# First modulation blocks split between TensorE and VectorE in a planned decoder block, with other costs in its planner

## The chip, the cores and the metric

The kernel runs on one core of a Trainium2 chip. The core has five instruction queues: TensorE (PE, matrix products; its weight loads are shown as PEld), VectorE (DVE), ScalarE (ACT), GpSimd (POOL) and SyncE (SP, which here only issues DMAs). Each queue works through its instructions in the order in which they were written; queues wait for one another by semaphores. The metric is the device time of one execution in microseconds, lower is better: the median of several runs.

## The reference

One decoder layer on 512 tokens of width 1024, all in float32, with one conditioning vector `c`:

```python
c_act = jax.nn.silu(c)
mod = c_act @ w_ada[l] + b_ada[l]                       # 1024 -> 6 * 1024
shift1, scale1, gate1, shift2, scale2, gate2 = split(mod, 6)
h = rms_norm(x, g_pre_mix[l]) * (1.0 + scale1) + shift1
y = token_mixer(h, ...)                                 # z = h @ w_in; conv branch, attention branch, merge
x = x + gate1 * rms_norm(y, g_post_mix[l])
h = rms_norm(x, g_pre_mlp[l]) * (1.0 + scale2) + shift2
y = square(relu(h @ w_mlp_in[l])) @ w_mlp_out[l]        # 1024 -> 4096 -> 1024
x = x + gate2 * rms_norm(y, g_post_mlp[l])
```

The six parts of `mod` are each a product of one vector of 1024 with a 1024 x 1024 matrix. Parts 0 and 1 (shift1, scale1) are needed before the first projection of the mixer can start, part 5 (gate2) only at the very end.

## The kernel before

All large products run on TensorE as three products of a split: each float32 operand is cut into a high part (rounded to float32r by a copy) and a low part (operand minus high part), and high x high, high x low, low x high are summed in PSUM (`mm3`, and the triple loop in `first_products`). So each weight block costs one copy on ScalarE (CAST in the profile) and one subtraction on VectorE (TENSOR_TENSOR), made by the class `W`, before its last third can run.

**The start of the kernel** is what most of the change touches. `x` comes in four row tiles of 512 KB; each is squared and summed on ScalarE, its reciprocal root is taken on GpSimd (a power of -0.5), and VectorE scales it. TensorE transposes the result in 32 blocks of 128 x 128 (4 per feature block, 8 feature blocks `k`), into one PSUM bank per feature block, and a copy brings each bank to `xnT`: the copies of the feature blocks in `XDVE` (L43; 1, 3, 5, 7) are on VectorE, those of the others on ScalarE (L636). The vector `c` is loaded after x, transposed on TensorE and turned into silu(c), the eight columns `cT`.

Then, for each of the eight feature blocks `k`, the kernel needs 128 columns of shift1 and of scale1. `ada_load` (L544) brings a block of 1024 x 2 x 128 weights (1 MB in 512-byte rows) by four DMAs of 256 KB. For `k` = 0 and 1 the sum over the 1024 inputs is made on TensorE, by eight float32 matmuls each with one column of `cT` as the weights (M = 1, N = 256); the row that comes out is copied by ScalarE and turned into columns by two more small matmuls and a transfer on VectorE (`to_columns`, L657). For `k` = 2 to 7 (the groups of `KGRP`) VectorE makes the sum: one TENSOR_SCALAR and seven SCALAR_TENSOR_TENSOR of 128 x 256, and `to_columns` then also adds over the partitions, with a vector of ones. `first_products` (L669) makes the modulated feature block (high part on ScalarE; a full-precision copy `v` on VectorE for `k` < `VDVE` = 2 and on ScalarE for the rest; low part on VectorE), splits the block of `w_in` that `g1_load` (L558) brought (128 rows x 896 columns, two DMAs), and issues 21 matmuls of 128 x 512 into seven PSUM banks.

**Late modulation.** Parts 2, 3, 4 and 5 are summed on VectorE beside other work, by the generator `ada_units` (L1167). A unit is one DMA of 1 MB and two VectorE instructions of 128 x 1024. `take(late, n)` advances it by n units. Part 5 (four units) is taken in the MLP. The MLP works in four quarters `ch` of 1024 hidden units (L1657); in each, the hidden units come in groups, most of them by a Strassen scheme (`strassen_in`), and their product with `w_mlp_out` by another (`strassen`). Before the change part 5 is taken from quarter 2 on: two units after each of the Strassen groups of that quarter (L1668), so all four units in quarter 2.

**What sets the order.** The program is first recorded as a list of operations (`record`), and then a list scheduler (`Planner.plan`, L325) simulates it with a cost for each operation (`cost`, L234, and a DMA's time in `record`). It decides the order in which each queue gets its instructions; this order is fixed in the program. TensorE takes the ready operation with the lowest rank, which is the place in the recorded list less `plan.boost`. The other queues take the ready operation with the earliest due time less `plan.hurry`. Due times are counted back from TensorE's order. `region` (L199) says which parts of a buffer an operation touches, as a range from the lowest to the highest word. Placement in the two SBUF arenas (`f_arena`, `r_arena`) and in the PSUM banks follows the simulated lifetimes, over up to 14 passes, and the pass with the shortest simulated length is issued. A buffer that is given to a new load must first be free, so placement also makes waits. The simulation holds SP back so that no more than `DEPTH` = 8 DMAs are under way.

All recorded instructions carry the line of one helper, L410, so groups of instructions are told apart by tiles and shapes.

Of the kernel before, what the change touches and what calls it, by code (L numbers as in the profile page):

```python
# [17 lines left out]
P = 128  # L18
# [23 lines left out]
CONV_DVE = ((0, 1), (2, 3), (4, 5), (6, 7))  # L42
XDVE = (1, 3, 5, 7)  # L43
VDVE = 2
TAIL = 2e4
# [6 lines left out]
ADAS = (1, 1, 0, 4)  # L52
KGRP = ((2,), (3,), (4,), (5,), (6,), (7,))
HX, HA, HG, HC = 1.2e5, 1e5, 3e3, 1.1e5
# [115 lines left out]
class Planner:  # L170
# [27 lines left out]
    @staticmethod  # L198
    def region(ap):  # L199

        t = ap.tensor
        dims = [list(d) for d in ap.ap]
        name = t.name.split("_bitcast")[0]
        row = dims[0][0]
        if row == 0 or len(t.shape) < 2 or "dram" in name or "spill" in name:
            return name, range(ap.offset, ap.offset + 1)
        if name.startswith("rows"):
            return name, range(ap.offset // row, ap.offset // row + dims[0][1])
        lo = ap.offset % row
        hi = lo + sum((n - 1) * s for s, n in dims[1:])  # L210
        u = 256 if name.startswith("psum") else 8 if "arena" in name else 1
        return name, range(lo // u, hi // u + 1)

# [20 lines left out]
    def cost(self, eng, fn, outs, ins, k):  # L234
# [17 lines left out]
        if eng == "dve":  # L252
            if fn in ("tensor_copy", "tensor_scalar"):
                return (1.04 if psum else 0.52) * n + 68 + 61 * scalars, 150.0
            if fn == "scalar_tensor_tensor":
                return 1.04 * n + 130, 150.0
            return 1.04 * n + 70, 150.0
        if fn == "memset":
            return 36.0, 100.0
        return (460.0 if ALU.pow in self.args else 160.0) + 1.0 * n, 150.0  # L260

    def record(self, eng, fn, a, k):
# [18 lines left out]
        if fn == "dma_start":  # L281
# [3 lines left out]
            n = min(self.run(outs[0]), self.run(ins[0]), 4096)  # L285
            o.dma = b * (13.0 + 0.0385 * n) / (16 * n) * (2 if eng == "pool" else 1)
        deps = set()
# [37 lines left out]
    def plan(self):  # L325
# [13 lines left out]
        heaps = {e: [] for e in self.NAMES}  # L339
        free = {e: 0.0 for e in self.NAMES}  # L340
        dma_free = 0.0
        landed = [0.0] * DEPTH
# [72 lines left out]
def tile_hybrid_block(  # L415
# [48 lines left out]
    def emit(past, replay):  # L464
# [72 lines left out]

        plan.hurry = HC
        c8 = tile_of([8, P], F32, "c8")
# [3 lines left out]

        def ada_load(ks):  # L544

# [3 lines left out]
            src = w_ada.rearrange("(j p) (s n) -> p s j n", p=P, s=6)  # L549
            step = KD // 2  # L550
            for j in range(0, KD, step):
                for s in range(2):
                    sp.dma_start(out=v[:, s, j:j + step], in_=src[:, s, j:j + step, ks[0] * P:ks[0] * P + n])
# [16 lines left out]
        plan.hurry = HA  # L570
        ada0 = ada_load((0,))
        plan.hurry = 0.0
# [83 lines left out]

        def to_columns(src, lp, ks):  # L657

            for s in range(2):
                for i, k in enumerate(ks):  # L660
                    pe.matmul(pb.v(bg)[:, s * KD + k:s * KD + k + 1], lhsT=src[:, s, i * P:(i + 1) * P], rhs=ones[0:lp, 0:1],
                              start=True, stop=True)
            ksl = slice(ks[0], ks[-1] + 1)
# [24 lines left out]

        plan.boost = 1000
        ad0 = [ada0]  # L690
        plan.hurry = HA - 1e4
        ad0.append(ada_load((1,)))
        wbs = []
        for k in range(2):
            plan.hurry = HA - (5e3 if k == 0 else 1.5e4)
            wbs.append(g1_load(k))
        plan.hurry = HG
        for k in range(2):
            av = ad0[k][1]
            ro = pb.v(bg)[0:1, 256:512].rearrange("p (s n) -> p s n", s=2)  # L700
            for j in range(KD):
                pe.matmul(ro, lhsT=cT[:, j:j + 1], rhs=av[:, :, j], start=j == 0, stop=j == KD - 1)
            fa.free(ad0[k][0])
            acc = fa.alloc(2 * P)
            accv = fa.v(acc, "p (s n) -> p s n", s=2)[0:1]
            act.copy(accv, ro)
            to_columns(accv, 1, (k,))
            fa.free(acc)
        plan.boost = 0
        plan.hurry = 0.0  # L710
        for k in range(2):
            first_products(k, wbs[k])

        for ks in KGRP:
            plan.hurry = HA - 1e4 * ks[0]
            n = len(ks) * P
            ab, av = ada_load(ks)
            ada_end = len(plan.ops) - 1
# [3 lines left out]
            plan.boost = 1000  # L722
            acc = fa.alloc(2 * n)
            accv = fa.v(acc, "p (s n) -> p s n", s=2)
            for j in range(KD):
                if j == 0:
                    dve.tensor_scalar(accv, av[:, :, 0], cT[:, 0:1], None, ALU.mult)
                else:
                    dve.scalar_tensor_tensor(accv, av[:, :, j], cT[:, j:j + 1], accv, op0=ALU.mult, op1=ALU.add)
            fa.free(ab)  # L730
            to_columns(accv, P, ks)
            fa.free(acc)
            plan.boost = 0
            plan.hurry = 0.0
            for k, wb in zip(ks, wbs):
# [921 lines left out]
        for ch in range(NCH):  # L1657
# [3 lines left out]
            for n0 in range(0, HPC, GRP):  # L1661
                if (ch, n0 - n0 % 4) in SIN:
                    if n0 % 4 == 0:
                        if not h2s_:
                            h2_sums()
                        strassen_in(hv, n0, (ch * HPC + n0) * P)
                        if ch >= NCH - 2:
                            take(late, 2 * ADAS[1])  # L1668
# [14 lines left out]
                for i in range(GRP):  # L1683
# [4 lines left out]
                    pb.free(bs[i])  # L1688
                if ch >= NCH - 2:
                    take(late, ADAS[1])  # L1690
# [110 lines left out]
```

## Time and profile before

| quantity | value |
|---|---|
| median of three runs | 815.28 us (814.91 to 816.14) |
| the profiled execution's own time | 812.54 us |
| its span, first to last instruction | 810.4 us |
| mean granted TensorE clock | 0.998 |
| TensorE matmul busy | 790.7 us, 4450 instructions |
| VectorE busy | 738.0 us |
| ScalarE busy | 472.0 us |
| GpSimd busy | 62.8 us |
| bytes moved by DMA | 131.00 MB, mean 162 GB/s |

Times in the views count from the start of the span. `out<-in` names the buffers that an instruction writes and reads; `128*1 128x256` on a matmul is the shape of its weights and of its moving operand. A float32 matmul is recorded as two instructions, a float32r matmul as one. Buffers of an arena all have the arena's name. "Idle before" is the time for which the engine stood still ahead of a group, with what ended it. A busy TensorE is not a TensorE at its peak, since the ends of matmuls are modelled: the number of matmuls in a stretch tells more.

### The profile page before, as it was taken

What the parts mean: (1) busy time and instruction counts of PE and PEld (TensorE: products, weight loads), DVE (VectorE), ACT (ScalarE), POOL (GpSimd) and SP (SyncE); (2) the same over time, 40 slices, a digit from 0 to 9 for tenths busy, and PEclk for the clock granted to TensorE, in tenths of its full rate; (3) what the DMA queues carried; (4) which work ended last, traced back from release to release, by engine and by line L of the source; (5) the groups of instructions that cost most, each with busy time, mean ns of one, the idle gap of its engine ahead of it and who ended that gap; (6) DMA issues with size and microseconds to landing.
All of it is one profiled execution on the core that took longest, in us unless ns stands there. A gap on an engine that the chain in (4) does not pass through costs nothing. (4 is left out here: it accounts for less than half of the span.)

```text
span 810.4 us, 11974 instructions
## 1 busy us (share of the span) xinstructions
PE 790.7 (98%) x4450; PEld 687.7 (85%) x4450; DVE 738.0 (91%) x1045; ACT 472.0 (58%) x784; POOL 62.8 (8%) x121
## 2 busy tenths in 40 slices
PE   6999999999999999999999999999999999999996
PEld 3778988889897888888888879988998899889985
DVE  3898999999999999999997579899689999996997
ACT  5455463365885247229243378677667756777851
POOL 2001010000000000000000021001002200320023
PEclk9999999999999999999999999999999999999999
DMA  9989433112352160064998044159317991895076
GB/s 295 313 247 341 144 116 110 53 53 66 105 170 78 53 202 5 1 222 162 344 391 281 7 159 148 53 149 266 132 53 157 243 343 37 171 288 178 28 164 134
DMA packets 99981, 131.00 MB, mean 162 GB/s; under 512 B 8433, under 2 KB 67154, under 8 KB 99922
## 3 DMA queue, kind: packets, MB, share of 16 engines
q1 hardware_dynamic: 93586, 118.69, 45.1%
q0 software_dynamic: 6336, 11.54, 8.9%
q8 instruction: 35, 0.57, 0.3%
q14 instruction: 24, 0.20, 0.1%
HBM read 109.23 MB, written 20.97 MB: 161 GB/s over the span
## 5 line engine op out<-in xcount | busy, mean ns | idle before, releaser
L410 PE MATMUL psum<-r_arena 128*128 128x512 f32 (+3 forms) x4108 | 751.1, 344 | 4.0 <-DVE f_arena L410 1.6
L410 PEld LDWEIGHTS psum<-r_arena 128*128 128x128 f32 x4108 | 647.6, 189 | 91.7 <-ACT r_arena L410 2.7
L410 ACT CAST r_arena<-f_arena 128x1024 fp32r<-128x1024 f32 (+5 forms) x249 | 235.2, 966 | 137.3 <-PE psum L410 86.4
L410 DVE TENSOR_TENSOR r_arena<-f_arena,r_arena 128x1024 fp32r<-128x1024 f32 (+5 forms) x259 | 276.1, 1093 | 28.0 <-PE psum L410 15.1
L410 DVE SCALAR_TENSOR_TENSOR f_arena<-f_arena,cw 128x512 f32<-128x512 f32 x240 | 164.2, 737 | 0.0
L410 DVE TENSOR_TENSOR f_arena<-f_arena 128x1024 f32<-128x1024 f32 (+3 forms) x108 | 113.6, 1071 | 4.7 <-ACT f_arena L410 2.4
L410 ACT ACTIVATE f_arena<-f_arena 128x512 f32<-128x512 f32 (+4 forms) x121 | 71.3, 607 | 42.9 <-DVE f_arena L410 42.0
L410 ACT COPY f_arena<-psum 128x512 f32<-128x512 f32 (+4 forms) x103 | 55.3, 547 | 41.5 <-PE psum L410 36.9
L410 DVE SCALAR_TENSOR_TENSOR f_arena<-f_arena,cT 128x256 f32<-128x256 f32 (+1 forms) x70 | 55.9, 800 | 1.2
L410 POOL DMA_DIRECT2D y_spill<-f_arena x40 | 34.8, 879 | 263.6 <-ACT f_arena L410 254.8
L410 ACT ACTIVATE f_arena<-psum 128x512 f32<-128x512 f32 x43 | 25.2, 593 | 45.4 <-PE psum L410 44.3
L410 PE MATMUL psum<-ident,f_arena 128*128 128x128 f32 (+1 forms) x234 | 34.8, 288 | 7.9 <-DVE f_arena L410 7.9
L410 PEld LDWEIGHTS psum<-ident,f_arena 128*128 128x128 f32 (+1 forms) x234 | 28.3, 147 | 14.0 <-DVE f_arena L410 9.3
L410 ACT CAST r_arena<-psum 128x512 fp32r<-128x512 f32 (+2 forms) x57 | 30.0, 562 | 12.7 <-PE psum L410 12.4
L410 DVE TENSOR_TENSOR r_arena<-psum,r_arena 128x512 fp32r<-128x512 f32 (+2 forms) x57 | 35.6, 653 | 0.9 <-ACT r_arena L410 0.6
L410 DVE TENSOR_TENSOR f_arena<-psum,f_arena 128x512 f32<-128x512 f32 (+1 forms) x34 | 22.3, 666 | 7.7 <-PE psum L410 7.6
L410 POOL TENSOR_TENSOR stats<-stats,nhalf 128x1 f32<-128x1 f32 (+1 forms) x17 | 15.5, 915 | 172.3 <-ACT stats L410 156.3
L410 POOL TENSOR_TENSOR lns<-lns,nhalf 128x4 f32<-128x4 f32 x1 | 1.4, 1400 | 249.5 <-DVE lns L410 249.5
L410 ACT ACTIVATE r_arena<-f_arena 128x256 fp32r<-128x256 f32 (+3 forms) x17 | 10.9, 642 | 14.4 <-DVE f_arena L410 11.3
L410 ACT ACTIVATE r_arena<-f_arena,mod 128x512 fp32r<-128x512 f32 x8 | 6.5, 816 | 21.6 <-DVE mod L410 21.6
L410 DVE TENSOR_SCALAR f_arena<-f_arena,stats 128x1024 f32<-128x1024 f32 x8 | 6.0, 753 | 13.6 <-POOL stats L410 13.6
L410 DVE CUSTOM_DVE_ANT_0 f_arena<-psum,mask 128x128 f32<-128x128 f32 (+3 forms) x32 | 14.6, 481 | 0.0
(98 smaller groups left out, 211.1 us busy)
## 6 DMA issues: line engine op xcount, KB each, us to landing
f_arena<-in_w_ada_dram SPq DMA_DIRECT2D x16, 1024.0 KB
f_arena<-in_w_mlp_in_dram SPq DMA_DIRECT2D x32, 512.0 KB
f_arena<-in_w_mlp_out_dram SPq DMA_DIRECT2D x32, 512.0 KB
f_arena<-in_w_in_dram SPq DMA_DIRECT2D x24, 512.0 KB
y_spill<-f_arena POOLq DMA_DIRECT2D x40, 256.0 KB, 6.2
f_arena<-in_w_ada_dram SPq DMA_DIRECT2D x32, 256.0 KB
f_arena<-in_x_dram SPq DMA_DIRECT2D x8, 512.0 KB
h_spill<-r_arena SPq DMA_DIRECT2D x16, 256.0 KB
```

The costliest lines, as they stand in the source:

```text
L410: getattr(self.real[o.eng], o.fn)(*o.a, **o.k)
```

## The change

Seven things are changed.

1. The sums of feature blocks 0 and 1 are shared. A new function `ada_sums` gives the weight rows `j` in `PE0` = 0, 2, 4, 6 (block 0) and `PE1` = 0, 1, 2 (block 1) to TensorE and the others (1, 3, 5, 7 and 3 to 7) to VectorE. `to_columns` takes a list of sources and adds them in PSUM, so it has four matmuls in place of two for these blocks. Blocks 2 to 7 keep the sum on VectorE. Block 1 moves into the common loop, so TensorE's part of it stands behind block 0's products in the recorded list, and only its `to_columns` is boosted.
2. `ada_load` for blocks 0 and 1 issues eight DMAs of 128 KB (one for each `j`, both halves) instead of four of 256 KB.
3. `c` is loaded ahead of x.
4. `XDVE` is empty and `VDVE` is 0: all eight copies of transposed x, and the full-precision modulated blocks 0 and 1, are on ScalarE.
5. The planner's costs of a 128 x 256 SCALAR_TENSOR_TENSOR, of the power on GpSimd, and of DMAs (plain and accumulating) are changed, and SP starts at 750 ns in the simulation.
6. `region` splits a strided access into its pieces, so that operations on different pieces are no longer taken to depend on one another.
7. `LATE5` = 1: part 5 is taken from quarter 1 on, so its four units are taken in quarter 1.

```diff
-XDVE = (1, 3, 5, 7)
-VDVE = 2
+XDVE = ()
+VDVE = 0
+PE0, CH0, PE1, CH1 = (0, 2, 4, 6), 1, (0, 1, 2), 1
+H1 = 3e3
+BOOST0 = 1000
+H0 = 2e4
-KGRP = ((2,), (3,), (4,), (5,), (6,), (7,))
+KGRP = ((1,), (2,), (3,), (4,), (5,), (6,), (7,))
+ADD, LATE5 = 2.6, 1
@@ region
-        hi = lo + sum((n - 1) * s for s, n in dims[1:])
         u = 256 if name.startswith("psum") else 8 if "arena" in name else 1
-        return name, range(lo // u, hi // u + 1)
+        at, inner = [lo], dims[1:]
+        while len(inner) > 1 and inner[0][0] >= 128 and inner[0][1] * len(at) <= 64:
+            s, n = inner.pop(0)
+            at = [a + i * s for a in at for i in range(n)]
+        ext = sum((n - 1) * s for s, n in inner)
+        return name, sorted({v for a in at for v in range(a // u, (a + ext) // u + 1)})
@@ cost, record, plan
-                return 1.04 * n + 130, 150.0
+                return 1.04 * n + (200 if n == 256 else 130), 150.0
-        return (460.0 if ALU.pow in self.args else 160.0) + 1.0 * n, 150.0
+        return (820.0 if ALU.pow in self.args else 160.0) + 1.0 * n, 150.0
-            o.dma = b * (13.0 + 0.0385 * n) / (16 * n) * (2 if eng == "pool" else 1)
+            o.dma = b * (6.0 + 0.040 * n) / (16 * n) * (ADD if eng == "pool" else 1)
+        free["sp"] = 750.0
@@ loads
-        plan.hurry = HC
+        plan.hurry = HX + 1e4
         c8 = tile_of([8, P], F32, "c8")
-        def ada_load(ks):
+        def ada_load(ks, step=KD // 2):
...
+                if step == 1:
+                    sp.dma_start(out=v[:, :, j], in_=src[:, 0:2, j, ks[0] * P:ks[0] * P + n])
+                    continue
-        ada0 = ada_load((0,))
+        ada0 = ada_load((0,), 1)
@@ sums
-        def to_columns(src, lp, ks):
+        def to_columns(srcs, ks):
             for s in range(2):
                 for i, k in enumerate(ks):
+                    for src, lp in srcs:
+                        pe.matmul(pb.v(bg)[:, s * KD + k:s * KD + k + 1], lhsT=src[:, s, i * P:(i + 1) * P],
+                                  rhs=ones[0:lp, 0:1], start=src is srcs[0][0], stop=src is srcs[-1][0])
+        plan.hurry = HA - 1e3
+        wbs = [g1_load(0)]
+        ro = pb.v(bg)[0:1, 256:512].rearrange("p (s n) -> p s n", s=2)
+        def ada_sums(ks, ada, on_pe=(), chains=1):
+            n = len(ks) * P
+            ab, av = ada
+            srcs, bufs = [], []
+            if on_pe:
+                bufs.append(fa.alloc(2 * P))
+                srcs.append((fa.v(bufs[0], "p (s n) -> p s n", s=2)[0:1], 1))
+            sums = []
+            at = 0
             for j in range(KD):
+                aj = av[:, :, j]
+                if j in on_pe:
+                    pe.matmul(ro, lhsT=cT[:, j:j + 1], rhs=aj, start=j == on_pe[0], stop=j == on_pe[-1])
+                    continue
+                if len(sums) < chains:
+                    bufs.append(fa.alloc(2 * n))
+                    sums.append(fa.v(bufs[-1], "p (s n) -> p s n", s=2))
+                    dve.tensor_scalar(sums[-1], aj, cT[:, j:j + 1], None, ALU.mult)
+                else:
+                    q = sums[at % chains]
+                    dve.scalar_tensor_tensor(q, aj, cT[:, j:j + 1], q, op0=ALU.mult, op1=ALU.add)
+                at += 1
+            fa.free(ab)
+            if on_pe:
+                act.copy(srcs[0][0], ro)
+            plan.boost = 1000
+            to_columns(srcs + [(q, P) for q in sums], ks)
+            fa.free(*bufs)
+            plan.boost = 0
+            plan.hurry = 0.0
+        plan.boost = BOOST0
+        plan.hurry = H0
+        ada_sums((0,), ada0, PE0, CH0)
+        first_products(0, wbs[0])
         for ks in KGRP:
             plan.hurry = HA - 1e4 * ks[0]
-            ab, av = ada_load(ks)
+            ada = ada_load(ks, 1 if ks[0] == 1 and PE1 else KD // 2)
...
+            if ks[0] == 1:
+                plan.hurry = H1
+                ada_sums(ks, ada, PE1, CH1)
+            else:
+                ada_sums(ks, ada)
@@ MLP, both places
-                        if ch >= NCH - 2:
+                        if ch >= LATE5:
                             take(late, 2 * ADAS[1])
```

More of the change, by code (lines that the diff above doesn't have):

```diff
@@ L549, in ada_load @@
             src = w_ada.rearrange("(j p) (s n) -> p s j n", p=P, s=6)
-            step = KD // 2
             for j in range(0, KD, step):
+                if step == 1:
+                    sp.dma_start(out=v[:, :, j], in_=src[:, 0:2, j, ks[0] * P:ks[0] * P + n])
+                    continue
                 for s in range(2):
@@ L655, in emit @@
         bg = bc
-        def to_columns(src, lp, ks):
+        def to_columns(srcs, ks):
             for s in range(2):
                 for i, k in enumerate(ks):
-                    pe.matmul(pb.v(bg)[:, s * KD + k:s * KD + k + 1], lhsT=src[:, s, i * P:(i + 1) * P], rhs=ones[0:lp, 0:1],
-                              start=True, stop=True)
+                    for src, lp in srcs:
+                        pe.matmul(pb.v(bg)[:, s * KD + k:s * KD + k + 1], lhsT=src[:, s, i * P:(i + 1) * P],
+                                  rhs=ones[0:lp, 0:1], start=src is srcs[0][0], stop=src is srcs[-1][0])
             ksl = slice(ks[0], ks[-1] + 1)
@@ L686, in first_products @@
             w.free()
[L689 to L700, printed above, removed]
-            for j in range(KD):
[L702 to L712, printed above, removed]
+        plan.hurry = HA - 1e3
[10 more added lines that the diff above has]
+            at = 0
+            for j in range(KD):
+                aj = av[:, :, j]
[18 more added lines that the diff above has]
+            plan.hurry = 0.0
@@ L714, in emit @@
+        plan.boost = BOOST0
+        plan.hurry = H0
+        ada_sums((0,), ada0, PE0, CH0)
+        first_products(0, wbs[0])
         for ks in KGRP:
             plan.hurry = HA - 1e4 * ks[0]
-            n = len(ks) * P
-            ab, av = ada_load(ks)
+            ada = ada_load(ks, 1 if ks[0] == 1 and PE1 else KD // 2)
             ada_end = len(plan.ops) - 1
@@ L722, in emit @@
             plan.boost = 1000
[L723 to L734, printed above, removed]
+            if ks[0] == 1:
[3 more added lines that the diff above has]
+                ada_sums(ks, ada)
             for k, wb in zip(ks, wbs):
@@ L1688, in emit @@
                     pb.free(bs[i])
-                if ch >= NCH - 2:
+                if ch >= LATE5:
                     take(late, ADAS[1])
```

## The prediction, made before the changed kernel was run

> **What bounds the kernel now.** I read the page first, then the engines' busy time by stretch, then TensorE's instructions in order of time.
>
> ```profile
> span 810.4 us, 11974 instructions
> PE 790.7 (98%) x4450; PEld 687.7 (85%) x4450; DVE 738.0 (91%) x1045; ACT 472.0 (58%) x784; POOL 62.8 (8%) x121
> ...
> 0.00:12.00 12.00, 4.59 (x20) 3.80 (x21) 2.89 (x8) 7.28 (x15) 5.14 (x49) 1.00 0.89 280
> 12.00:24.00 12.00, 11.62 (x59) 5.55 (x57) 6.85 (x11) 5.25 (x9) 0.75 (x2) 1.00 1.14 318
> 24.00:64.00 40.00, 39.91 (x186) 31.90 (x186) 36.92 (x82) 18.03 (x24) 0.68 (x6) 1.00 0.98 284
> 260.00:280.00 20.00, 20.00 (x90) 16.58 (x89) 20.00 (x28) 5.77 (x7) 0.00 (x0) 1.00 0.26 76
> 540.00:600.00 60.00, 60.00 (x405) 55.75 (x404) 48.81 (x44) 41.34 (x53) 3.50 (x5) 1.00 0.61 181
> 620.00:680.00 60.00, 58.90 (x400) 54.73 (x399) 55.95 (x52) 40.58 (x52) 8.39 (x10) 1.00 0.84 240
> 800.00:812.00 12.00, 2.79 (x22) 2.38 (x20) 6.52 (x14) 0.81 (x3) 1.55 (x2) 0.82 0.65 147
> ```
>
> The columns of the stretches are length, then PE, PEld, DVE, ACT and POOL busy with counts, granted clock, DMA share, GB/s. TensorE is idle for 19.7 us in all (810.4 - 790.7), 7.4 of them before its first instruction, so what shortens the kernel is less work on TensorE or an earlier start of useful work. At its best it runs 90 matmuls in 20 us (260 to 280), 222 ns each. Here is its beginning:
>
> ```profile
> 7.41 1.76 PE L410 MATMUL psum<-ident,f_arena 128*128 128x128 f32 x7 [7.41 <-DVE f_arena L410]
> 13.30 3.61 PE L410 MATMUL psum<-f_arena,cT 128*1 128x256 f32 x16
> 17.65 0.60 PE L410 MATMUL psum<-ones,f_arena 1*128 1x1 f32 x4
> 18.18 0.59 PE L410 MATMUL psum<-f_arena,cT 128*1 128x256 f32 x2
> 20.80 1.89 PE L410 MATMUL psum<-f_arena,cT 128*1 128x256 f32 x8
> 22.62 1.20 PE L410 MATMUL psum<-r_arena 128*128 128x512 f32 x4
> 24.27 7.10 PE L410 MATMUL psum<-r_arena 128*128 128x512 f32 x30
> 31.58 5.52 PE L410 MATMUL psum<-r_arena 128*128 128x512 f32 x23
> 53.06 0.50 PE L410 MATMUL psum<-ones,f_arena 128*128 128x1 f32 x4
> 53.42 5.19 PE L410 MATMUL psum<-r_arena 128*128 128x512 f32 x21
> 58.45 0.50 PE L410 MATMUL psum<-ones,f_arena 128*128 128x1 f32 x4
> 58.81 6.79 PE L410 MATMUL psum<-r_arena 128*128 128x512 f32 x27
> ```
>
> The first product runs at 22.62; until then TensorE does transposes and 16 modulation matmuls (32 records). 34 of the 168 first products are done at 31.4, so block 1's last (the 42nd) is done near 33.4 (8 more at 0.25 us). From there each feature block takes 5.39 us (53.06 to 58.45), where 21 matmuls at 222 ns and the 0.36 us of the transfer (53.06 to 53.42) would be 5.02: these matmuls take 247 ns, with VectorE busy 36.92 of 40 us. The eighth block ends near 64.1 (21 of the last 27). Behind it TensorE has hardly a gap, and one that bears on the change, at 661.64, is below.
>
> **1. The shared sums, on TensorE.** Nine of sixteen modulation matmuls leave TensorE. Eight took 3.61 us, so that is -4.06 us. Each of blocks 0 and 1 gets two more small matmuls in the transfer; two take 0.53 us (17.65 to 18.18), so +1.06. Net -3.0 us of TensorE work: with TensorE full from 12 us on, the lower bound of the gain, if nothing else moves.
>
> **2. The same, as a chain.** The start is earlier by more than that, because block 1's matmuls now stand behind block 0's products and no longer ahead of them (20.80 to 22.62). I build block 0's new chain from these rows:
>
> ```profile
> 0.74 1.81 SPq L410 DMA_DIRECT2D f_arena<-in_x_dram  x4
> 2.60 0.39 SPq L410 DMA_DIRECT2D c<-in_c_dram  x1
> 8.15 0.37 SPq L410 DMA_DIRECT2D f_arena<-in_w_ada_dram  x1
> 9.77 0.92 SPq L410 DMA_DIRECT2D f_arena<-in_w_ada_dram  x2
> SPq L410 <- DMA f_arena<-in_x_dram: 4.0, 4, 2.1
> 4.39 1.06 ACT L410 ACTIVATE r_arena<-f_arena 128x1024 fp32r<-128x1024 f32 x1 [2.06 <-DMA f_arena<-in_x_dram]
> 29.71 1.00 DVE L410 SCALAR_TENSOR_TENSOR f_arena<-f_arena,cT 128x256 f32<-128x256 f32 x2
> 32.07 0.82 ACT L410 ACTIVATE r_arena<-f_arena,mod 128x512 fp32r<-128x512 f32 x1 [5.65 <-DVE mod L410]
> 32.79 0.80 ACT L410 ACTIVATE f_arena<-f_arena,mod 128x512 f32<-128x512 f32 x1
> ```
>
> SP waits four times for tiles of x: its ninth DMA is issued only when an earlier one lands, so eight are in flight. Its issues at 8.15 and 9.77 follow the third and fourth tile of x. With c ahead, x lands about 0.4 later (0.39 for c's issue): the last tile at 10.2. Block 0's 1.05 MB at 318 GB/s take 3.3 us more, 13.5. Its pieces are half as large, so eight in flight hold less; after the last tile of x lands three pieces have still to be issued, for which I add 0.5: 14.0. VectorE's last sum takes 0.5, and from the end of a sum to the modulated block on ScalarE it is 1.36 us (30.71 to 32.07), then 0.82: first product near 16.9, against 22.62.
>
> **3. ScalarE's load** goes against this. Empty `XDVE` and `VDVE` = 0 give it work that VectorE did:
>
> ```profile
> 13.08 1.07 ACT L410 COPY f_arena<-psum 128x512 f32<-128x512 f32 x2 [1.83 <-PE psum L410]
> 19.91 1.76 ACT L410 CAST r_arena<-f_arena 128x896 fp32r<-128x896 f32 x2
> 22.78 0.36 ACT L410 COPY f_arena<-psum 1x256 f32<-1x256 f32 x1 [1.10 <-PE psum L410]
> 19.19 0.55 DVE L410 TENSOR_SCALAR f_arena<-f_arena,mod 128x512 f32<-128x512 f32 x1
> 20.91 0.69 DVE L410 COPY f_arena<-psum 128x512 f32<-128x512 f32 x1 [0.17 <-PE psum L410]
> ```
>
> From the last transposes (13.5) it has eight copies of 0.54, the row copy 0.36, the weight split 0.93, the block 0.82 and its full copy 0.80: 7.2 us, to 20.7. The first products need all seven banks that the transposes hold, and the low part needs the full copy, so block 0's products are stretched to 21.5-22.5, not 16.9 + 21 x 0.222 = 21.6 in every case. Block 1 adds three matmuls (1.35), the transfer (0.9) and 21 products (4.67): its last product at 27 (when the small ones fall into the stretched time) to 29.4, against 33.4. Gain 4.0 to 6.4.
>
> **4. VectorE and the feed after that.** VectorE gets 9 sums (4.3 us) and loses four copies (4 x 0.69) and two full copies (2 x 0.55), 3.9: +0.4 us, hidden in the 5.2 us that it idled between 12 and 24. Then nothing of blocks 2 to 7 changes; between 5.39 (VectorE's pace) and 5.02 us a block (TensorE's), the six blocks gain 0 to 2.2 more. The feed allows it: 1.51 MB a block at 318 GB/s is 4.7 us. All of the start together: 3.0 by work alone, 6.4 by the chain, more only if both ends of steps 3 and 4 fall well. I take 4.8, nearer the chain, since TensorE's order lets it fill the stretched time with the transposes and small matmuls that are left.
>
> **5. Half-size pieces, by a rule.** By the Trainium skill, DMA: Bandwidth & Descriptors, section "Measured (HBM→SBUF, 128 partitions, SWDGE, issued from GpSimd)", transfers should be batched to 1 MiB: 64 KB takes 0.95 us and 1 MB 6.15 us; interpolated, as an estimate, eight pieces of 128 KB would take 2.4 us more than four of 256 KB, and the gain would nearly go for the two blocks. The 318 GB/s here, with pieces of 256 KB or less in flight together, speaks against adding them up one by one.
>
> **6. Part 5 in quarter 1.** The chain of waits shows what it does in quarter 2, and the list of TensorE's waits the price:
>
> ```profile
> 633.21 7.31 DMA f_arena<-in_w_ada_dram
> 643.65 10.34 DMA f_arena<-in_w_mlp_in_dram
> 661.64 93.01 PE psum L410 x623
> PE psum L410 <- DVE f_arena L410: 1.1, 1, 1.1
> ```
>
> A load of 1 MB lands, VectorE uses it, only then its buffer is free for a load of `w_mlp_in`, and TensorE stalls 1.1 us at 660.5. Quarter 2 is rid of this (-1.1). Quarter 1 gets 4 MB more: its stretch moved 181 GB/s over 60 us against 240, so with them it is as loaded as quarter 2 was, and VectorE's 11.2 idle us there must take the sums (it was busy 55.95 us in quarter 2's stretch against 48.81 here, so some 7 us of them). The stall can return there, 0 to 1.1 or, if two follow each other, more. I take -0.3 net, between -1.1 and +0.8.
>
> **7. Costs, `region`, SP's start.** They add no instruction; they move orders and places everywhere. No row prices that. TensorE's idle time between 24 and 800 is about 4.3 us (19.7, less 7.4 at the start, 0.4 from 12 to 24 and 7.6 behind 800), so they can win at most some of it; I take 0, and 1 us either way in the range.
>
> **Sum.** 812.54 is the profiled execution's time (span 810.4); -4.8 - 0.3 + 0 = 807.4. That execution lies 2.7 us under the median shown, so on the median's footing it is 815.28 - 5.1 = **810.2 us**. Its own range: -6.4 - 1.1 - 0.3 to -3.0 + 0.8 + 0.2, 807.5 to 813.3.
>
> **Rivals.**
> *The feed starves.* Half-size pieces behind eight-in-flight: if a5 to a7 and block 1's eight pieces are issued one by one as earlier ones land (0.43 us each, the last tile of x at 10.2, and 3.65 us from issue to landing as for the first tile of x, 0.74 to 4.39), block 0 is complete at 15.2 instead of 14.0 and block 1 later by as much again. Gain 4.8 - 2.4 = 2.4, with 0.3 from part 5: 812.6, and with ScalarE's copies late as well about 813.5. For: SP waits on x already. Against: DMAs moved 280 GB/s over the first 12 us and 318 over the next. The page's rule would lead to about the same place, near 815.
> *Hidden anyway.* VectorE is at 20.00 of 20 us at 260 to 280 with the convolution; if it is what sets the pace there, the early gain is lost: 815.0. Against: TensorE runs at its best 222 ns there, and VectorE too starts blocks 2 to 7 earlier.
> *Part 5 lands on the path (slower).* In quarter 1 the first load of `w_mlp_in` behind a unit gets its buffer only after that unit's sum. Once TensorE's lead is under the unit's landing time, each unit costs what is not covered: 7.31 us for the row above, of which quarter 2 showed only 1.1, since TensorE was that far ahead. Uncovered it is 815.28 - 4.8 - 1.1 + 7.31 = 816.7; two such units give 823. It decides from 4.8 us of stall. For: VectorE is as full in quarter 1 with the sums as it was in quarter 2. Against: 79 us earlier there are fewer accumulating DMAs on GpSimd (3.50 us busy against 8.39).
>
> **Chances.** Forecast 0.64; feed 0.14 (two thirds of it still faster by 0.2%, which is 1.6 us and about what a measurement can tell from no change); hidden 0.07; slower 0.15. So faster 0.74, same 0.11, slower 0.15. The range 806.8 to 816.7 adds the move of orders below, and above the feed, the hidden case and half of the slower one, so that about 0.15 is left out.
>
> **What would show it.** Right: the first 128x512 product near 17 us, the eighth block's end near 59, 18 modulation records fewer and 8 small ones more on TensorE, no wait of 1.1 us near 660, and the same interval from the eighth block to the end as before (746 us). Step 2 is wrong if c's load or a blocked VectorE delays the last tile of x beyond 13 us; step 3 if ScalarE is full from 13 to 24 and TensorE waits for copies; step 4 if blocks 2 to 7 take over 5.4 us each; step 6 if TensorE waits between 540 and 600. The forecast as a whole is wrong if the end of the eighth block moves and the end of the kernel does not follow.

## The result, and the profile after

The changed kernel takes 818.63 us (median of seven runs, 817.76 to 819.88), the kernel before 815.64 in the same session: a ratio of 1.0052, 95% interval 1.0040 to 1.0063. It is slower by 3.0 us between the medians (the ratio would make it 4.2), where 5.1 us faster was forecast, and lies above the predicted range.

First the page of the changed kernel and its engines' busy time by stretch, in the columns used before (length, then PE, PEld, DVE, ACT, POOL busy with counts, granted clock, DMA share, GB/s).

```profile
span 818.1 us, 11960 instructions
PE 793.6 (97%) x4440; PEld 687.8 (84%) x4440; DVE 737.2 (90%) x1048; ACT 478.1 (58%) x790; POOL 60.7 (7%) x121
...
0.00:20.00 20.00, 11.68 (x53) 6.60 (x54) 7.03 (x17) 11.16 (x22) 5.86 (x49) 1.00 0.84 264
20.00:40.00 20.00, 18.48 (x82) 13.52 (x81) 16.93 (x39) 11.34 (x17) 0.50 (x4) 1.00 1.14 316
560.00:580.00 20.00, 18.94 (x127) 17.23 (x126) 19.32 (x18) 12.88 (x17) 2.18 (x3) 1.00 1.06 341
660.00:680.00 20.00, 20.00 (x169) 20.00 (x168) 12.86 (x12) 13.35 (x19) 0.00 (x0) 1.00 0.11 33
700.00:720.00 20.00, 17.25 (x73) 13.88 (x72) 15.65 (x14) 13.60 (x17) 6.04 (x7) 0.95 0.98 233
```

TensorE's idle time near 660 is gone (20.00 busy from 660 to 680), as forecast. In its place TensorE now loses time from 20 to 40, at 565 and at 715. Its beginning, in order of time:

```profile
7.82 1.76 PE L420 MATMUL psum<-ident,f_arena 128*128 128x128 f32 x7 [5.30 <-DVE f_arena L420]
10.92 1.87 PE L420 MATMUL psum<-f_arena,cT 128*1 128x256 f32 x4
15.32 0.59 PE L420 MATMUL psum<-f_arena,cT 128*1 128x256 f32 x2
20.43 0.73 PE L420 MATMUL psum<-r_arena 128*128 128x512 f32 x2
21.61 1.68 PE L420 MATMUL psum<-r_arena 128*128 128x512 f32 x5
24.39 8.00 PE L420 MATMUL psum<-r_arena 128*128 128x512 f32 x34
32.59 0.48 PE L420 MATMUL psum<-r_arena 128*128 128x512 f32 x1
34.01 1.88 PE L420 MATMUL psum<-r_arena 128*128 128x512 f32 x7 [0.94 <-ACT r_arena L420]
36.48 0.96 PE L420 MATMUL psum<-r_arena 128*128 128x512 f32 x3 [0.59 <-DVE r_arena L420]
57.76 8.47 PE L420 MATMUL psum<-r_arena 128*128 128x512 f32 x36
```

The last modulation matmul of block 0 starts at 15.32, the first product at 20.43 (22.62 before), but only seven products are done when the full run begins at 24.39 (24.27 before, with four done). From 32.2 to 37.3 there are eleven. The 168 first products (132 ahead of the last row, 36 in it) end at 66.2.

VectorE's share of block 0's sum ends at 14.09, so its weights had landed by then. ScalarE begins the modulated block at 19.05, 5.0 us later:

```profile
13.09 1.00 DVE L420 SCALAR_TENSOR_TENSOR f_arena<-f_arena,cT 128x256 f32<-128x256 f32 x2
15.95 0.36 ACT L420 COPY f_arena<-psum 1x256 f32<-1x256 f32 x1 [4.77 <-PE psum L420]
17.67 0.90 PE L420 MATMUL psum<-ones,f_arena 128*128 128x1 f32 x6
18.67 0.16 DVE L420 TENSOR_TENSOR mod<-psum,cols 128x1 f32<-128x1 f32 x1 [2.67 <-PE psum L420]
19.05 0.81 ACT L420 ACTIVATE r_arena<-f_arena,mod 128x512 fp32r<-128x512 f32 x1
```

In between come TensorE's share (to 15.9), ScalarE's copy of its row, the small matmuls (to 18.6) and VectorE's transfer. TensorE does its part of this among transposes, of which 21 of 32 start behind 13.4 and the last ends at 20.0.

To tell the start from the rest I count TensorE's float32r matmuls in order of time, in each profile, and note when the 42nd, 84th and 168th start (the end of blocks 1, 3 and 7) and how long it is from the 168th to the 4108th of 4116 (the last eight, in the kernel's tail, are left out), as differences of times rounded to 0.1 us. In before they start at 33.3, 43.9 and 65.2, and 736.9 us follow; in after at 32.6, 45.3 and 65.8, and 744.0 follow. So the profile shows 0.6 us lost by the end of the first products, and the rest behind them. The two profiled executions overstate the difference: before's is 3.1 us under its median (812.54 against 815.64), after's 1.2 over (819.88 against 818.63). Taking that off the 7.7 us between the spans leaves 3.3, about what the medians show.

Two further places show where time goes. The feed, over the first 30 us, of before and then of after:

```profile
DMA packets 11992, 9.04 MB, mean 301 GB/s; under 512 B 523, under 2 KB 10967, under 8 KB 11991
```
```profile
GB/s 0 0 44 257 350 404 382 393 393 382 309 342 287 145 173 248 180 236 343 254 276 329 223 264 321 296 323 296 336 312 316 361 334 296 292 290 305 337 364 310
DMA packets 10997, 8.48 MB, mean 283 GB/s; under 512 B 620, under 2 KB 9972, under 8 KB 10996
...
4.19 6.90 SPq L420 DMA_DIRECT2D f_arena<-in_w_ada_dram  x8
9.70 1.40 SPq L420 DMA_DIRECT2D f_arena<-in_w_ada_dram  x3
30.60 0.94 ACT L420 CAST r_arena<-f_arena 128x896 fp32r<-128x896 f32 x1 [3.23 <-DMA f_arena<-in_w_in_dram]
```

Each number of the GB/s row is 0.75 us. From 9.75 to 13.5 it falls to 145-248: SP issues three of the eight small DMAs of block 0 only from 9.70, when the last tile of x has landed. At 30 us the feed is 0.56 MB behind, 1.8 us at its rate, and ScalarE waits 3.23 us for a block of `w_in` (a wait of the same length stays, 1 us earlier, when the pieces are 256 KB again, in e_four below).

And the MLP's last quarter in the changed kernel: SP's issues, the chain of waits, TensorE's wait, and the granted clock behind it.

```profile
701.12 17.47 SPq L420 DMA_DIRECT2D f_arena<-in_w_mlp_in_dram  x7
SPq L420 <- DVE r_arena L420: 49.1, 8, 30.6
705.65 10.06 DMA f_arena<-in_w_mlp_in_dram
718.25 4.11 PE L420 MATMUL psum<-r_arena 128*128 128x512 f32 x10 [2.75 <-DVE r_arena L420]
...
718.00:720.00 2.00, 1.75 (x4) 1.46 (x5) 2.00 (x3) 0.00 (x0) 0.71 (x1) 0.54 1.11 252
720.00:722.00 2.00, 2.00 (x7) 1.53 (x7) 2.00 (x3) 0.00 (x0) 0.00 (x0) 0.60 0.91 236
722.00:724.00 2.00, 2.00 (x10) 1.65 (x9) 1.87 (x2) 0.81 (x2) 0.49 (x1) 1.00 0.89 221
```
```profile
693.73 15.69 SPq L410 DMA_DIRECT2D f_arena<-in_w_mlp_in_dram  x7
```

The seven loads of `w_mlp_in` for this stretch start at 701.12, where before (last row) they started at 693.73, because the buffers that they were given come free later (SP waited up to 30.6 us for VectorE to be done with one, 20.6 in before). Some 3 of these 7.4 us are the lag that TensorE already has there: its 3401st float32r matmul starts at 684.5 against 681.4. A load takes 10.06 us to land there. TensorE stands still for 2.75 us, and then runs at a granted clock of 0.54 to 0.60 for some 4 us: four and seven matmuls in 2 us, where ten is full speed.

### The profile page after: what moved, and what is told of

The parts are those of the page before. It is cut to its first block, busy times and chain, and to the rows that moved or that the text cites. A ratio compares the mean times of both kernels' runs of the same rounds, so it can differ in the third digit from the quotient of the medians.

```text
span 818.1 us, 11960 instructions
## 1 busy us (share of the span) xinstructions
PE 793.6 (97%) x4440; PEld 687.8 (84%) x4440; DVE 737.2 (90%) x1048; ACT 478.1 (58%) x790; POOL 60.7 (7%) x121
## 4 chain that ended last, share of the span: by engine, by line
PE 77%; DVE 10%; ACT 4%; DMA 4%; issue 3%; POOL 1%; SPq 0%; DVEq 0%; POOLq 0%; ACTq 0%
PE psum L420 77%; DVE f_arena L420 5%; DVE r_arena L420 4%; ACT f_arena L420 3%; ACT r_arena L420 2%; DMA y_spill<-f_arena 2%; DMA f_arena<-in_w_mlp_in_dram 1%; DMA rows<-in_g_pre_mix_dram 1%; POOL stats L420 1%; SPq L420 0%; DVEq L1817 0%; POOLq L1817 0%; ACT stats L420 0%; DVE mod L420 0%; DVEq L420 0%
## 5 line engine op out<-in xcount | busy, mean ns | idle before, releaser
L420 ACT CAST r_arena<-f_arena 128x1024 fp32r<-128x1024 f32 (+4 forms) x249 | 235.9, 965 | 167.7 <-PE psum L420 111.6
L420 ACT COPY f_arena<-psum 128x512 f32<-128x512 f32 (+4 forms) x107 | 57.6, 550 | 46.6 <-PE psum L420 37.9
L420 DVE SCALAR_TENSOR_TENSOR f_arena<-f_arena,cT 128x256 f32<-128x256 f32 (+1 forms) x77 | 57.9, 770 | 1.6 <-DMA f_arena<-in_w_ada_dram 0.7
L420 ACT ACTIVATE f_arena<-f_arena,lnh 128x512 f32<-128x512 f32 x16 | 12.3, 811 | 2.6 <-DVE f_arena L420 2.5
```

The source lines that it names most:

```text
L420: getattr(self.real[o.eng], o.fn)(*o.a, **o.k)
```

## The experiments

All times are of runs on the same chip as the runs of the kernel before that they are compared with; the ratio is to those. "42nd", "84th", "168th" and "rest" are the marks of the section above, each from one profile.

| kernel | 42nd | 84th | 168th | rest | ratio to before (95%) |
|---|---|---|---|---|---|
| before | 33.3 | 43.9 | 65.2 | 736.9 | 1 |
| after | 32.6 | 45.3 | 65.8 | 744.0 | 1.0052 (1.0040-1.0063) |
| f_late: before, part 5 in quarter 1 | 33.8 | 44.4 | 65.7 | 738.1 | 1.0002 (0.9986-1.0017) |
| f_plan: before, new costs and regions | 33.8 | 44.3 | 65.0 | 739.3 | 1.0023 (1.0011-1.0035) |
| f_start: new start, old planner | 68.6 | 78.1 | 97.1 | 739.8 | 1.0399 (1.0385-1.0412) |
| f_start_plan: after, part 5 in quarter 2 | 32.3 | 45.0 | 65.6 | 740.3 | 1.0054 (1.0038-1.0069) |
| e_four: after, 256 KB pieces | 31.2 | 43.0 | 63.6 | 738.0 | 0.9982 (0.9969-0.9994) |
| e_actb: after, copies back on VectorE | 32.9 | 45.3 | 66.2 | 738.4 | 1.0033 (1.0012-1.0053) |
| e_nudge_before: before, one cost +1 ns | 34.1 | 44.7 | 66.0 | 740.0 | 1.0022 (1.0009-1.0036) |
| e_nudge_after: after, the same | 32.5 | 45.2 | 65.7 | 739.3 | 1.0033 (1.0022-1.0045) |
| g_eight_before: before, 128 KB pieces | 33.6 | 44.1 | 66.1 | 735.6 | 0.9997 (0.9988-1.0006) |
| g_all_pe: e_four, nothing shared | 35.3 | 45.8 | 66.4 | 736.4 | 1.0023 (1.0009-1.0037) |
| g_four_actb: e_four, copies back | 35.9 | 46.5 | 67.0 | 743.6 | 1.0101 (1.0077-1.0124) |
| g_four_nudge: e_four, one cost +1 ns | 31.6 | 43.5 | 64.0 | 739.6 | 1.0007 (0.9999-1.0016) |

Each mark is from one execution. f_late and e_nudge_before, whose start is not edited, have the 168th product 0.5 and 0.8 us later than before, so a difference of less than about 1 us between marks shows nothing by itself; by this measure the start of the changed kernel (+0.6) is not told apart from that of before. The executions of one kernel lie up to 10 us apart (e_actb, 813.76 to 823.54), so the rest of a single one has to be read beside the medians.

### Which part of the change costs

Four kernels with parts of the change: part 5 alone, the planner alone, the start alone, and start with planner.

```diff
 f_late, on before
-                        if ch >= NCH - 2:
+                        if ch >= 1:
 f_plan, on before: region, cost, o.dma and free["sp"] as in the change, nothing else
 f_start, on after: region, cost, o.dma and free["sp"] as before, and
-ADD, LATE5 = 2.6, 1
+ADD, LATE5 = 2.6, 2
 f_start_plan, on after
-ADD, LATE5 = 2.6, 1
+ADD, LATE5 = 2.6, 2
```

> The kernel before with part 5 taken from quarter 1 on, nothing else changed. Theory A (part 5's place is what costs): TensorE gains a stall of 1 us near 565 and one of 2 to 3 us near 715, the one near 660 is gone; 2 to 3 us slower than before. Theory B (the planner's new costs and regions move the buffers of the MLP): no such pair of stalls; the stall at 660 is only moved, within 1 us of before. Theory C (the start): the first products end at 65.5 as before.

> The kernel before with the planner's new costs, the split regions and SP's start, nothing else changed; the instructions are the same, only their order and the buffers' places can differ. Theory A (part 5): within 1 us of before. Theory B: 2 to 3 us slower, with new stalls of TensorE behind loads of w_mlp_in between 540 and 760. If the new costs were better ones: 0.5 to 1 us faster.

> The changed start alone (shared sums, 128 KB pieces, c first, copies on ScalarE), with the old planner and part 5 from quarter 2 on. Theory C (eight DMAs in flight hold too few bytes in 128 KB pieces, the feed runs 1.8 us behind by 30 us and takes the start's whole gain): the first products end at 65.5 to 66.5, the kernel is 0 to 1 us slower than before, with the MLP as it was. Rival (the start is a gain and only the plan spoils it): first products end below 63, and 2 us or more faster than before.

> The changed kernel with part 5 back in quarter 2. Theory A (part 5): the 2.75 us stall near 715 and the one near 565 are gone, 2 to 3 us faster than the changed kernel, 815.5 to 816.5. Theory B: the stalls in the MLP stay at 2 us or more in sum, 818. Either way the first products end near 66 as in the changed kernel.

Part 5 alone makes no difference (1.0002), and putting it back makes none either (1.0054 beside 1.0052). TensorE's busy time of f_late, in the stretches where the theory wanted stalls:

```profile
580.00:600.00 20.00, 19.14 (x160) 18.94 (x159) 19.34 (x18) 13.84 (x19) 0.00 (x0) 1.00 0.45 150
700.00:720.00 20.00, 20.00 (x90) 16.56 (x89) 19.09 (x17) 14.75 (x18) 6.19 (x8) 1.00 1.04 264
```

There is 0.9 us idle in quarter 1 and none at 715. Theory A falls: the stall at 715 does not come from where part 5 is taken. f_start_plan too still has a stall there, 1.4 us at 711; its rest is 3.7 us shorter than the changed kernel's in the profile, which the medians do not bear out.

The planner alone costs 0.23%, in the rest and not in the start, though without the new stalls that theory B asked for (no idle time of TensorE above 0.9 us), so theory B is not excluded by this run; the nudges below bear on it.

The start alone was far from both theories: 4% slower, 31.9 of some 33 us in the start. TensorE's waits in its first 60 us and SP's issues say why.

```profile
PE psum L415 <- DMA f_arena<-in_w_ada_dram: 25.4, 3, 10.5
...
3.03 0.75 SPq L415 DMA_DIRECT2D f_arena<-in_w_ada_dram  x1
4.71 0.40 SPq L415 DMA_DIRECT2D f_arena<-in_w_ada_dram  x1
5.15 4.04 SPq L415 DMA_DIRECT2D f_arena<-in_w_in_dram  x4
9.25 3.17 SPq L415 DMA_DIRECT2D f_arena<-in_w_ada_dram  x6
12.47 1.07 SPq L415 DMA_DIRECT2D f_arena<-in_w_in_dram  x2
```

The small pieces of block 0 are no longer issued together: they are spread over later rounds of loads, and TensorE, which must add them in order, waits 10.5 us twice and 4.5 once. The likely reason is that each piece is a strided slice whose old region, lowest to highest word, overlaps the other pieces, so the old planner lets one wait for another. The split regions are then part of what the small pieces need; regions and costs were not put back separately.

### The feed

```diff
 e_four, on after
-        ada0 = ada_load((0,), 1)
+        ada0 = ada_load((0,))
-            ada = ada_load(ks, 1 if ks[0] == 1 and PE1 else KD // 2)
+            ada = ada_load(ks)
 e_actb, on after
-XDVE = ()
-VDVE = 0
+XDVE = (1, 3, 5, 7)
+VDVE = 2
 g_eight_before, on before: the split regions, and for blocks 0 and 1
+                if step == 1:
+                    sp.dma_start(out=v[:, :, j], in_=src[:, 0:2, j, ks[0] * P:ks[0] * P + n])
+                    continue
```

> The changed kernel with the weights of blocks 0 and 1 loaded by four DMAs of 256 KB each as before, all else as changed. Theory C1 (eight small DMAs in flight starve the feed): the DMAs move 2 MB or more by 30 us like the kernel before (301 GB/s over the first 30 us against 283), block 2's first products are not held up, and the 84th product starts at 43 or earlier, 2 us before the changed kernel's 45.3. Rival (ScalarE's copies hold up the start): the 84th product stays at 45 or later.

> The changed kernel with four copies of transposed x and the two full-precision blocks back on VectorE, all else as changed. Rival theory (ScalarE's copies hold up the start): the 21st product starts 1.5 us or more earlier than the changed kernel's 27.5, and the 84th before 44. Theory C1 (the feed): the first products may come up to 1 us earlier, but block 2 waits for its w_in block as in the changed kernel, and the 84th product stays within 0.6 us of 45.3.

> The kernel before with the weights of blocks 0 and 1 in eight DMAs of 128 KB each, and the split regions that the planner needs for such pieces; sums, copies and costs as before. Theory C1 (the small pieces starve the feed): less than 8.6 MB moved by 30 us (9.04 before), the 84th product 1 us or more later than before's 43.9. Rival (the feed fell behind for another reason of the changed start): 8.9 MB or more, the 84th product within 0.5 us of before.

The feed and TensorE's start of e_four:

```profile
GB/s 0 0 38 246 344 410 382 371 377 388 346 336 331 294 290 330 356 326 292 292 292 307 354 343 300 292 290 300 326 359 319 292 292 290 334 337 335 307 294 293
DMA packets 11927, 9.00 MB, mean 300 GB/s; under 512 B 522, under 2 KB 10902, under 8 KB 11926
...
19.15 1.20 PE L420 MATMUL psum<-r_arena 128*128 128x512 f32 x4
20.82 1.22 PE L420 MATMUL psum<-r_arena 128*128 128x512 f32 x4 [0.47 <-ACT f_arena L420]
23.37 7.07 PE L420 MATMUL psum<-r_arena 128*128 128x512 f32 x30
32.06 1.88 PE L420 MATMUL psum<-r_arena 128*128 128x512 f32 x7 [0.47 <-ACT r_arena L420]
29.61 0.94 ACT L420 CAST r_arena<-f_arena 128x896 fp32r<-128x896 f32 x1 [3.26 <-DMA f_arena<-in_w_in_dram]
```

With pieces of 256 KB the feed is back at 300 GB/s (290 to 356 from 9.75 to 13.5), the 84th product starts at 43.0, and the 168th 2.2 us earlier than in the changed kernel and 1.6 earlier than before. That is what the feed theory asked for (but for its 2 MB by 30 us, a bar that tells nothing: the changed kernel moved 8.48). Since the size of the pieces is all that was edited, it shows their cost; that too few bytes in flight are the reason is argued from SP's rows. The kernel as a whole is faster than before (0.9982). With the copies back on VectorE instead, the 84th stays at 45.3: ScalarE's copies are not what holds up the start.

In the old start the same small pieces slow the feed too (8.63 MB by 30 us), but the 84th product stays within 0.2 us, where the feed theory asked for less than 8.6 MB and 1 us or more: here its forecast missed. The 168th is 0.9 us later, by a wait of 1.1 us at 55. The likely reason is that the old start reaches its blocks later and does not need the feed so early; no run tells this apart from other differences between the two starts.

### What the sharing is worth

```diff
 g_all_pe, on e_four
-PE0, CH0, PE1, CH1 = (0, 2, 4, 6), 1, (0, 1, 2), 1
+PE0, CH0, PE1, CH1 = (0, 1, 2, 3, 4, 5, 6, 7), 1, (0, 1, 2, 3, 4, 5, 6, 7), 1
 g_four_actb, on e_four: XDVE = (1, 3, 5, 7), VDVE = 2
```

> The changed kernel with four DMAs of 256 KB for blocks 0 and 1 and with both sums wholly on TensorE, so nothing is shared; block 1's matmuls still behind block 0's products. Theory E (VectorE is what paces blocks 1 to 3, so the work that the sharing gives it undoes what it takes from TensorE): the 84th product at 43 or earlier, no later than with sharing. Rival (TensorE's work is what counts, -3.0 us by nine matmuls fewer): the 84th product 2 us or more later than with sharing, 45 or more.

> The changed kernel with four DMAs of 256 KB for blocks 0 and 1 and with four copies and the two full blocks back on VectorE. If ScalarE's copies stretch block 0's products once the feed is mended: the 21st product at 25 or earlier (26.0 with them on ScalarE). If VectorE paces blocks 1 to 3: the 84th product no earlier than 43.0, or later.

Without sharing the 84th and the 168th product start 2.8 us later (45.8 against 43.0, 66.4 against 63.6). Theory E falls: the nine matmuls that leave TensorE count almost in full. What stays of the start's change without sharing and without small pieces (c first, block 1's matmuls behind block 0's products, copies on ScalarE) costs 1.2 us against before (66.4 against 65.2), not much more than unedited starts differ by; its parts were not separated.

With the copies back on VectorE the 21st product comes no earlier (26.6 against 26.0) and the 42nd 4.7 us later. Some 1.7 us of that, half of 3.41 us, goes to a stretch from 29.46 in which the trace has TensorE's granted clock at 0.5. In the changed kernel the same move (e_actb) shifts the marks from the 42nd on by 0.4 us or less. So moving the copies to ScalarE pays in e_four; that VectorE cannot make sums and copies in time is the likely reason, but not shown.

### The plan

One cost of the planner, that of a VectorE instruction with two tensors, is raised by 1 ns.

```diff
 e_nudge_before on before, e_nudge_after on after, g_four_nudge on e_four
-            return 1.04 * n + 70, 150.0
+            return 1.04 * n + 71, 150.0
```

> The kernel before, with one cost of the planner raised by 1 ns (a VectorE instruction of two tensors), which says nothing new of the chip. Theory D (the plan's chance: any other cost makes another plan, and plans differ by some us in the MLP): the time differs from before by 0.5 to 4 us, with stalls of TensorE in other places after 480. Theory B (the new costs are worse than the old as such): within 0.5 us of before.

> The changed kernel, with the same cost raised by 1 ns. Theory D: the 4.6 us that the changed kernel lost around 715 change by 1.5 us or more either way, while the first 168 products keep their time within 1 us (66). Theory B: the losses at 490, 560 and 715 stay where they are, and the kernel is 2.5 to 3.5 us slower than before.

> The changed kernel with four DMAs of 256 KB for blocks 0 and 1, and the cost of a VectorE instruction of two tensors raised by 1 ns in the planner. Theory D (the plan's chance moves the MLP by some us): the first 168 products end within 0.5 us of the unnudged 63.6, and the stretch from there to the end differs from its 738.0 us by 1 us or more. Rival (that version's plan is a better one as such): the stretch stays within 0.5 us and the kernel 1 to 1.5 us faster than before.

A nanosecond that says nothing of the chip makes the kernel before 0.22% slower: as much as the new costs do, and two fifths of what the whole change does by the ratios. Its start is 0.8 us later, and what it loses behind that is mainly one stall of 3.7 us in the MLP, where before has 1.1 us:

```profile
640.00:660.00 20.00, 16.26 (x121) 15.55 (x120) 15.60 (x15) 10.90 (x14) 1.88 (x3) 0.98 1.06 329
```

On the changed kernel the same nudge leaves the start as it was (65.7) and shrinks the loss at 715, while another appears at 630:

```profile
560.00:580.00 20.00, 20.00 (x146) 18.84 (x145) 18.88 (x18) 12.45 (x16) 0.86 (x1) 1.00 1.05 343
620.00:640.00 20.00, 18.76 (x82) 14.78 (x81) 17.69 (x16) 13.69 (x17) 6.62 (x8) 1.00 1.05 265
700.00:720.00 20.00, 19.00 (x84) 15.14 (x83) 17.84 (x16) 13.96 (x17) 6.04 (x7) 1.00 1.06 268
```

On e_four it leaves the start within 0.4 us and takes 1.6 us of the rest. Over the fourteen kernels the rest runs from 735.6 to 744.0 us, and it does not go with any one part of the change: g_eight_before has a shorter one than before, g_all_pe about the same, after and g_four_actb the longest. These are single executions, but the medians agree: what is left of their difference to before when the start's is taken off runs from -1.2 us (g_eight_before) to 5.4 us (g_four_actb). Theory D holds. Whether the new costs are on the whole better or worse than the old stays open: their 1.0023 cannot be told from the nudge's 1.0022, and the nine plans made with them average 739.9 us in the rest, the five made with the old ones 738.1.

## Why the prediction was wrong

The start was forecast at -4.8 us and measured at +0.6: that is 5.4 of the 8.1 us between the forecast (-5.1) and the medians (+3.0). It is steps 2 to 4 that fail there, and step 7 behind it.

**Step 1 (less TensorE work) was right**: -3.0 forecast, 2.8 us measured by g_all_pe against e_four. The reading beside it had a slip: the last 27 matmuls of my list all belong to the first products (4 + 30 + 23 + 4 x 21 + 27 = 168), so these ended at 65.6 and not at 64.1.

**Step 2 (the earlier chain) failed in the term from the end of the sum to the modulated block.** I took 1.36 us, from a later block whose sum VectorE makes alone. In block 0, TensorE's share and its small matmuls stand among transposes and the row goes over ScalarE: 5.0 us (14.09 to 19.05), and still 4.15 in e_four (13.65 to 17.80). So the first product came at 20.43, in e_four at 19.15, and not near 16.9. The weights of block 0 were not late: I had them complete at 14.0, and VectorE's last sum began at 13.60. The feed's term, 0.5 us for half-size pieces, was too small too, but further on: the feed fell 1.8 us behind by 30 us, and mending it is worth 2.2 us at the 168th product. The rival in which the feed starves had 2.4 us for this, and I gave it a chance of only 0.14; its path, block 0 complete only at 15.2, did not come about, so that its price is near the measured one is in part luck.

**Steps 3 and 4 (gain of 4.0 to 6.4 at block 1, nothing after it gets worse) failed.** Step 3 counted from the last transposes at 13.5, but before itself has seven of its 32 behind that (six at 16.85, one at 20.54), and in the changed kernel they run to 20.0. The end of block 0's products, set at 21.5 to 22.5, came later: the 21st starts at 27.5, in e_four at 26.0. The 42nd starts 0.7 us earlier than before, 2.1 in e_four. "The feed allows it: 4.7 us a block" compared rates and left out the date: at 30.60 ScalarE still waits 3.23 us for a block's weights (3.26 in e_four). From the 42nd to the 84th product it takes 12.7 us in after and 11.8 in e_four, against 10.6 before, so a part of any lead is given back. What step 3 feared from ScalarE's load is not the loss: with the copies back on VectorE the start is no faster (e_actb, g_four_actb).

Put together, the start: -2.8 (sharing) + 2.2 (small pieces) + 1.2 (the rest of the start's moves) = +0.6 us. The three are the steps from before over g_all_pe and e_four to after, so they must add up to the measured 65.8 against 65.2; the sum confirms none of them.

**Step 5 (the rule of the Trainium skill, DMA: Bandwidth & Descriptors, section "Measured (HBM→SBUF, 128 partitions, SWDGE, issued from GpSimd)")**: the estimate from its table, 2.4 us more for a block of eight pieces than of four and double that for two, is above the 2.2 us that the small pieces cost at the 168th product here; but it points the right way. They cost nothing at the 84th product in the old start.

**Step 6 (part 5)** was near enough: -0.3 forecast, -0.2 between the medians of f_late, with an interval from -1.1 to +1.4 us. The stall at 660 went and others came, but its going bears step 6 out only by luck: it is gone as well in f_plan and f_start_plan, which leave part 5 in quarter 2. The slower rival built on part 5 is refuted by f_late, which is no slower, and by f_start_plan, where part 5 is back in quarter 2 and the kernel is as slow.

**Step 7 (costs, `region`, SP's start) is the step that fails on the sign.** I took 0 with 1 us either way (the sum's own range has only 0.3 and 0.2 of it), since TensorE had only 4.3 us of idle time to win; I did not see that the loss has no such bound. Changed costs moved the MLP's stalls in every plan tried here, and the plans differ by up to 8.4 us in their profiles. With the start at +0.6, about 2.4 us of the 3.0 lost between the medians are behind it (3.6 by the ratio): in the changed kernel's profile at 490, 565 and 715. Why the planner's new plan is slow in just these places stays open. The forecast passed an early gain through 740 us of unchanged plan, and the plan was not unchanged. None of my rivals said this. The tell-tale that I had named, the eighth block moving and the end not following, is what e_four shows: its 168th product starts 1.6 us earlier than before's, its 4108th float32r matmul 0.5.

## What to carry to other kernels

Where a scheduler inside the kernel writes the order and the buffers' places, any edit draws a new plan for the whole kernel: price that draw first, by moving a meaningless cost by a nanosecond, and judge an edit by the time at which its own stage ends. When a chain is priced from rows of another block, check that the block takes the same engines in the same order: here TensorE's queue put transposes between the links. When a load is cut into smaller DMAs, count the bytes in flight, not the bytes a second, and ask when each block's data must have landed. Of the versions run here, the changed kernel with 256 KB pieces beats both (0.9982 of before), though its nudged twin only draws level with before (1.0007), so a part of that is the plan too.

## What the runs showed of the hardware

I had not expected what a stall of TensorE costs beyond itself. After the 2.75 us of idle time at 715 the granted clock was 0.54 and 0.60 in the next two stretches of 2 us, and the stretch from the 3401st to the 3601st float32r matmul took 46.6 us against 42.0 before: 4.6 us lost, not 2.75 (an estimate from the rows: 2.75 idle and half of the 3.41 us at half the clock, named below, make 4.5). In the kernel before the 1.1 us at 660 left the clock at 1.00:

```profile
660.00:662.00 2.00, 0.90 (x8) 0.70 (x7) 2.00 (x3) 0.38 (x1) 0.00 (x0) 1.00 1.02 388
662.00:664.00 2.00, 2.00 (x19) 2.00 (x18) 2.00 (x3) 1.83 (x3) 0.00 (x0) 1.00 0.74 254
```

The trace's record of the granted clock has this stall's 0.5 from 718.17, for 3.41 us. Stretches of the same 3.41 us at 0.5 stand in the records of f_start (from 689.99), e_four (480.76), e_nudge_before (659.35) and g_four_actb (29.46 and 718.95). In the 3.41 us ahead of each of the six TensorE was still busy for 0.73 to 2.19 us, and in e_four no single idle time there was above 0.72 us: several short waits close together were enough. Where the line runs stays open, since 1.89 us of work in such a stretch of before (from 800.9) left the clock at 1.00.

The Trainium skill, TensorE: Matmul & The Clock Gate, section "What's actually happening", has the clock halved after at least one idle window of about 3.4 us; the halved clock agrees with the rows, while here the window ahead was not idle throughout. Its budget for coming back, also about 3.4 us of work, agrees with the stretches of 3.41 us.
